# A hybrid attention layer on one core: q and k of the forgetting attention stored as two planes, high and low

## The chip, the cores and the metric

The kernel runs on one core of one Trainium2 chip. The metric is the device time of one launch in microseconds (us); smaller is better. The engines of a core that matter here are TensorE (PE; its weight loads are listed apart as PEld), VectorE (DVE), ScalarE (ACT), GpSimd (POOL) and SyncE (SP). A transfer between device memory and the core's SBUF is issued by one of the engines: `nc.sync` by SP, `nc.scalar` by ACT, `nc.gpsimd` by POOL. Matrix products accumulate in PSUM tiles of 128x512.

## The reference

One layer of a decoder with sequence length and width 1024 and float32 throughout. The cut below keeps what is computed:

```python
h = rms_norm(x, g);  proj = h @ w_in
o_a = softmax-merge over 3 groups of dilated_window_attention(...)  # 12 heads, width 64
logits = (q @ k.T) * 64**-0.5 + (c[t] - c[s]); mask s <= t           # 8 forgetting heads
o_b = softmax(logits) @ v                   # c = cumulative sum of log_sigmoid(f)
x = x + (sigmoid(gate_a) * (o_a @ w_dil_out) + sigmoid(gate_b) * (o_b @ w_fox_out)) @ w_out
x = x + (silu(h2 @ w_up1) * (h2 @ w_up2)) @ w_down                   # h2 = rms_norm(x), 2816 wide
out = rms_norm(x, g_final)
```

## The kernel before, in words

**Every product is three.** A float32 operand is held as a pair of fp32r tiles: a high part, which ScalarE makes by a copy, and a low part, which VectorE makes as the source less the high part (`split`, lines 94 to 96). A product of pairs is high times high, high times low and low times high (`mm3`, lines 98 to 101, and `prod`, line 272, whose matmul is line 276).

**Stages**, with their place in the profile. Norm, values and combinations of the normalized input's quadrants (`T1` to `T4`): up to some 137 us. **Block products**, to some 264 us: six calls of `projections` (line 279), four for q and k of the forgetting heads (a pair of heads is a block of 128 columns, and a call makes two blocks) and two for dilated heads. A call multiplies two column blocks of weights by the input with seven block products of 12 matmuls instead of eight, by the scheme of Strassen and Winograd: `left_side` (line 252) takes two raw weight tiles, `rg` and `ru` (tag `wr`, 2 buffers, loaded on SP at line 243), and makes the pairs A1 (of `rg`), S12 and S34 (from sums formed on GpSimd in tiles `s`) and A22, the second half of `ru` (tag `a22`). The products' sums are joined into two tiles `qo` (128x1024, 3 buffers), and these are stored to device memory by GpSimd (line 314), those of the forgetting heads to `fqk_dram`. The same `left_side` serves the FFN later.

**Forgetting attention**, some 290 to 503 us, two heads at a time, each in two halves of queries. `fox_qk` (line 550) makes a pair's operands: for each head, and for q and for k, it loads the head's 64 rows from `fqk_dram` twice, into rows 0 to 63 and 64 to 127 of a tile `qraw` (2 buffers; line 558, SP); ScalarE copies it to the high part (line 559; q times the factor `SCALE`), and VectorE subtracts (lines 563 and 566). `qx` then holds the high part of q in both halves, `kx` the high part of k in one half and its low part in the other, and `ql` the low part of q in one half and zeros in the other. A score is `kx`·`qx` (high and low k by high q) plus `kx`·`ql` (line 583). `fox_scores` writes logits to `L` on ScalarE (L587), takes maxima on VectorE and one over all keys on GpSimd; `fox_exp` subtracts (VectorE) and exponentiates (ScalarE); `fox_values` multiplies with the values and, by a product with ones, makes the denominators. The scores of a unit of work are issued ahead of the values of the unit before.

**Late projections** (`ahead`, line 214): 24 calls, 8 for the remaining dilated q and k (to `dqk_dram`) and 16 for the gates (to `g_dram`). A call loads 128 weight columns and splits them (`wr`, `wh`, `wl`), makes 48 products into two PSUM tiles `pf` (lines 99 to 101, tag `f`, 2 banks), copies them on ScalarE to a tile `fst` (line 224, 2 buffers), and stores that on ScalarE's queue (line 225). The last call is held behind the last value product of the dilated attention:

```python
with tc.issue_after(last_pv[0].ins) if i == 2 * KT - 1 else ExitStack():
    ahead(fpool, GATE0 + n * P, g_dram[n])
```

**Dilated attention**, some 510 to 651 us, in the same steps; its exponentials are ScalarE L750 to L756, its value products L780 and its denominators L783. **Merge**, from some 668 us: attention outputs are loaded into tiles `land` and split into `oh` and `ol` (`load_o`, by lines 95 and 96), then come the products with `w_fox_out` and `w_dil_out` (L189 and following), `w_out`, the FFN and the last norm, to the end at 1520 us.

**What sets the order.** No order is written out by hand. The program is written as a sequence of instructions, and a scheduler simulates the engines and puts each engine's instructions into one fixed order; tags and buffer numbers of the pools say what must wait for what. Products of `ahead` stand between attention steps wherever that simulation put them.

Of the kernel before, what the change touches and what calls it, by code (L numbers as in the profile page):

```python
# [8 lines left out]
F32 = mybir.dt.float32  # L9
# [6 lines left out]
P = 128  # L16
# [31 lines left out]
def layer_kernel(  # L48
# [152 lines left out]

    g_dram = dpool.tile([2 * KT, P, S], F32, name="g_dram")

    fqk_dram = dpool.tile([2, 4, P, S], F32, name="fqk_dram")
    vf_dram = dpool.tile([NT, P, FOX_W], F32, name="vf_dram")
    dqk_dram = dpool.tile([2, 3, 2, P, S], F32, name="dqk_dram")
    vd_dram = dpool.tile([3, NT, P, 256], F32, name="vd_dram")
# [38 lines left out]
    def pair_of(raw):  # L246

        w = Pair(*[wpool.tile([P, KT, P], F32R, tag="w" + n, name=nm("w" + n), bufs=2) for n in "hl"])
        split(w.hi[:], w.lo[:], raw)
        return w  # L250

    def left_side(pool, rg, ru, bufs):

        def pair(k, tag, bufs):
            return Pair(*[pool.tile([P, k, P], F32R, tag=tag + n, name=nm("w" + n), bufs=bufs) for n in "hl"])

        def fill(w, raw):
            split(w.hi[:], w.lo[:], raw)
            return w

        g1, g2, u1, u2 = rg[:, :4], rg[:, 4:], ru[:, :4], ru[:, 4:]
        S34, A22, A1 = pair(KT, "s34", 1), pair(4, "a22", 2), pair_of(rg[:])
        s12 = pool.tile([P, KT, P], F32, tag="s", name=nm("s12"), bufs=2)
        nc.gpsimd.tensor_tensor(out=s12[:, :4], in0=u1, in1=u2, op=ALU.add)  # L264
        nc.gpsimd.tensor_tensor(out=s12[:, 4:], in0=s12[:, :4], in1=g1, op=ALU.subtract)  # L265
        S12 = fill(pair(KT, "s12", bufs), s12[:])
        s34 = pool.tile([P, KT, P], F32, tag="s", name=nm("s34"), bufs=2)
        nc.gpsimd.tensor_tensor(out=s34[:, :4], in0=g1, in1=u1, op=ALU.subtract)
        nc.gpsimd.tensor_tensor(out=s34[:, 4:], in0=g2, in1=s12[:, 4:], op=ALU.subtract)
        return A1, S12, fill(S34, s34[:]), fill(A22, u2)  # L270
# [5 lines left out]
                last_mm[0] = nc.tensor.matmul(bank[:], p, q, start=first and k == 0 and n == 0,  # L276
                                              stop=k == 3 and n == 2, skip_group_check=True)

    def projections(pool, T, c, dst, dls, sc):

        T1, T2, T3, T4 = T
        o1, o2 = [pool.tile([P, dl, S // dl], F32, tag="qo", name=nm("qo"), bufs=3) for dl in dls]
# [28 lines left out]
        prod(b3, S34[:, 4:], B22)  # L311
        join(o1[:, :, n1:], b3, v2, dls[0])
        for o, d in zip((o2, o1), dst[::-1]):
            nc.gpsimd.dma_start(out=d, in_=o[:].rearrange("p r i -> p (r i)"))

    LAG = 3
    merge_order = []
# [90 lines left out]
    with pool_of("comb1", 1) as tpool:  # L408
# [90 lines left out]
        with pool_of("proj", 1) as upool:  # L499
            cums = [upool.tile([P] + d, F32, name=n, bufs=1) for n, d in (  # L500
                ("sums", [2, P]), ("az", [NT * 8]), ("u", [NT * 8]), ("t1", [NT * 8]), ("tot", [NT, 8]))]
            for pr in range(0, 4, 2):
                for a in range(2):
                    c0 = FOX0 + a * FOX_W + pr * P
                    projections(upool, T, (c0, c0 + P), [fqk_dram[a, pr + i] for i in range(2)], (1, 1), 1.0)
                if pr == 0:
                    decay(*cums)
            for two in TWOS:
                projections(upool, T, [dil_cols(*t) for t in two], [dqk_dram[t] for t in two],
                            [STR[a][g] for u, g, a in two], (SCALE, 1.0)[two[0][2]])  # L510
# [35 lines left out]
    with pool_of("fox", 1) as spool:  # L546
# [3 lines left out]
        def fox_qk(pool, ql, pr):  # L550

            qx = [pool.tile([P, S], F32R, tag=f"qx{e}", name=nm("qx"), bufs=1) for e in range(2)]
            kx = [pool.tile([P, S], F32R, tag=f"kx{e}", name=nm("kx"), bufs=1) for e in range(2)]
            for a, xs, sc in ((0, qx, SCALE), (1, kx, 1.0)):
                for e in range(2):
                    raw = pool.tile([P, S], F32, tag="qraw", name=nm("qraw"), bufs=2)
                    for at in half:
                        nc.sync.dma_start(out=raw[at, :], in_=fqk_dram[a, pr, half[e], :])
                    nc.scalar.activation(out=xs[e][:], in_=raw[:], func=AF.Copy, scale=sc)
                    rows = half[e] if a == 0 else half[1 - e]  # L560
                    hi = xs[e][rows, :].bitcast(F32)
                    if a == 0:
                        nc.vector.scalar_tensor_tensor(out=ql[e][rows, :], in0=raw[rows, :], scalar=sc, in1=hi,
                                                       op0=ALU.mult, op1=ALU.subtract)
                    else:
                        nc.vector.tensor_tensor(out=xs[e][rows, :], in0=raw[rows, :], in1=hi, op=ALU.subtract)
            return qx, ql, kx

        def fox_scores(pool, qk, h, b):
# [72 lines left out]
        with pool_of("foxa", 2) as apool:  # L642
            pend = None
            ql = [apool.tile([P, S], F32R, name=f"ql{e}", bufs=1) for e in range(2)]
            for e in range(2):
                nc.gpsimd.memset(ql[e][half[1 - e], :].bitcast(F32), 0.0)
            for pr in range(4):
                qk = fox_qk(apool, ql, pr)
                for b in range(2):
                    unit = [fox_scores(apool, qk, 2 * pr + e, b) for e in range(2)], pr, b  # L650
                    if pend:
                        fox_values(apool, *pend)
                    pend = unit
            fox_values(apool, *pend)
# [431 lines left out]
```

## Time and profile before

| | us |
|---|---|
| median of 3 runs | 1523.96 (1522.74 to 1524.77) |
| the profiled execution | 1522.51 |
| its span in the profile | 1520.2 |
| TensorE busy | 1472.8, 97% of the span |
| VectorE busy | 894.1, 59% |
| ScalarE busy | 536.8, 35% |

The profiled execution's time is 2.3 us more than its span, which is taken from the first to the last recorded instruction. The mean granted clock of TensorE is 0.992 of full speed. In the slices of 38 us below (each digit tenths of a slice; PEclk the granted clock), TensorE is full nearly throughout. The slices under 9 are the first, two that hold the end of the dilated attention and the start of the merge (608 to 684 us), and the last:

```profile
## 2 busy tenths in 40 slices
PE   7999999999999999789999999999999999999997
PEld 6899888867777777568888788888888877888886
DVE  6482433398898399936628854444444445856546
ACT  5232221476566132335315432222222225312113
POOL 1012321273353011100000155555555553140000
PEclk9999999999999999989999999999999999999999
```

### The profile page before, as it was taken

How to read it: one execution, taken by the hardware profiler on the slowest of the kernel's cores; microseconds unless marked ns; L12 is line 12 of the kernel's file. 1: busy time of each engine (PE TensorE's matmuls, PEld its weight loads, DVE VectorE, ACT ScalarE, POOL GpSimd, SP SyncE). 2: the span in 40 equal slices, each digit the busy share in tenths (PEclk: the TensorE clock that was granted, in tenths of full speed). 3: DMA queues.
4: the chain of work that ended last, by engine and by line, in shares of the span. 5: the costliest groups of instructions: out<-in, count | busy, mean ns of one | idle time of the engine just before them, and what ended most of it. 6: DMA issues, size and time to landing. Idle time of an engine off the chain costs nothing.

```text
span 1520.2 us, 18124 instructions
## 1 busy us (share of the span) xinstructions
PE 1472.8 (97%) x6956; PEld 1192.0 (78%) x6956; DVE 894.1 (59%) x1321; ACT 536.8 (35%) x808; POOL 418.4 (28%) x351
## 2 busy tenths in 40 slices
PE   7999999999999999789999999999999999999997
PEld 6899888867777777568888788888888877888886
DVE  6482433398898399936628854444444445856546
ACT  5232221476566132335315432222222225312113
POOL 1012321273353011100000155555555553140000
PEclk9999999999999999989999999999999999999999
DMA  8132334733332732155613122222222225642202
GB/s 257 42 98 63 111 97 121 226 113 102 110 99 69 257 122 66 56 181 180 242 56 139 42 69 84 83 83 83 84 83 83 84 97 197 204 139 84 96 15 97
DMA packets 139045, 171.60 MB, mean 113 GB/s; under 512 B 6992, under 2 KB 108368, under 8 KB 138960
## 3 DMA queue, kind: packets, MB, share of 16 engines
q1 hardware_dynamic: 118096, 105.95, 23.5%
q0 software_dynamic: 9616, 34.62, 6.1%
q10 hardware_dynamic: 11248, 29.89, 5.3%
q8 instruction: 54, 0.88, 0.2%
q14 instruction: 31, 0.25, 0.1%
HBM read 123.25 MB, written 47.19 MB: 112 GB/s over the span
## 4 chain that ended last, share of the span: by engine, by line
PE 85%; DMA 4%; DVE 3%; ACT 3%; POOL 3%; issue 2%; SPq 0%; ACTq 0%; POOLq 0%; DVEq 0%
PE pd L276 26%; PE pd L99 10%; PE pd L100 10%; PE pd L101 10%; PE pf L100 5%; PE pf L101 5%; PE pf L99 5%; DMA wr<-in_w_ffn_in_dram 2%; PE pd L189 2%; PE pd L634 2%; PE pd L190 2%; PE pd L193 2%; ACT wh L95 2%; POOL sg L994 1%; PE pd L780 1%
## 5 line engine op out<-in xcount | busy, mean ns | idle before, releaser
L96 DVE TENSOR_TENSOR wl<-wr,wh 128x1024 fp32r<-128x1024 f32 (+2 forms) x152 | 165.9, 1095 | 147.3 <-ACT wh L95 146.7
L95 ACT ACTIVATE wh<-wr 128x1024 fp32r<-128x1024 f32 (+2 forms) x152 | 140.6, 932 | 316.2 <-PE pd L100 91.9
L276 PE MATMUL pd<-hT_t,wh 128*128 128x512 f32 x784 | 242.2, 390 | 1.4 <-ACT cc L289 0.7
L276 PE MATMUL pd<-tT,wh 128*128 128x512 f32 x672 | 206.9, 389 | 0.4 <-DVE v L909 0.4
L276 PEld LDWEIGHTS pd<-hT_t,wh 128*128 128x128 f32 x784 | 147.0, 188 | 32.4 <-ACT c L977 1.1
L276 PE MATMUL pd<-hT_t,wl 128*128 128x512 f32 x392 | 153.9, 393 | 1.7 <-DVE wl L96 1.5
L99 PE MATMUL pf<-hT_t,wh 128*128 128x512 f32 x384 | 151.0, 393 | 0.6 <-ACT fst L224 0.6
L100 PE MATMUL pf<-hT_t,wh 128*128 128x512 f32 x384 | 151.0, 393 | 0.0
L101 PE MATMUL pf<-hT_t,wl 128*128 128x512 f32 x384 | 150.9, 394 | 0.0
L276 PEld LDWEIGHTS pd<-tT,wh 128*128 128x128 f32 x672 | 126.1, 188 | 27.0 <-DVE v L909 0.8
L99 PE MATMUL pd<-wh,wh 128*128 128x512 f32 x352 | 137.6, 392 | 3.4 <-DVE acc L1037 1.9
L100 PE MATMUL pd<-wl,wh 128*128 128x512 f32 x352 | 137.1, 389 | 0.0
L101 PE MATMUL pd<-wh,wl 128*128 128x512 f32 x352 | 137.0, 389 | 0.0
L276 PE MATMUL pd<-tT,wl 128*128 128x512 f32 x336 | 130.1, 390 | 0.0
L1037 DVE TENSOR_TENSOR acc<-pd,acc 128x512 f32<-128x512 f32 x128 | 85.6, 685 | 69.2 <-PE pd L101 69.1
L264 POOL TENSOR_TENSOR s<-wr 128x512 f32<-128x512 f32 x26 | 38.9, 1496 | 312.8 <-DVE tT L96 196.0
L96 DVE TENSOR_TENSOR wl<-s,wh 128x1024 fp32r<-128x1024 f32 x52 | 64.7, 1246 | 66.6 <-ACT wh L95 63.7
L95 ACT ACTIVATE wh<-s 128x1024 fp32r<-128x1024 f32 x52 | 55.1, 1060 | 126.5 <-POOL s L265 95.1
L276 PEld LDWEIGHTS pd<-hT_t,wl 128*128 128x128 f32 x392 | 73.6, 188 | 22.2 <-DVE wl L96 7.3
L101 PEld LDWEIGHTS pf<-hT_t,wl 128*128 128x128 f32 x384 | 72.1, 188 | 19.8 <-issue 5.0
L99 PEld LDWEIGHTS pf<-hT_t,wh 128*128 128x128 f32 x384 | 72.1, 188 | 19.7 <-issue 4.6
L100 PEld LDWEIGHTS pf<-hT_t,wh 128*128 128x128 f32 x384 | 72.1, 188 | 18.5 <-issue 4.1
(228 smaller groups left out, 2776.8 us busy)
## 6 DMA issues: line engine op xcount, KB each, us to landing
wr<-in_w_in_dram SPq DMA_DIRECT2D x46, 512.0 KB, 4.3
wr<-in_w_ffn_in_dram SPq DMA_DIRECT2D x44, 512.0 KB, 4.3
wr<-a_dram SPq DMA_DIRECT2D x22, 512.0 KB, 4.3
wr<-in_w_ffn_down_dram SPq DMA_DIRECT2D x22, 512.0 KB, 3.7
a_dram<-a POOLq DMA_DIRECT2D x20, 512.0 KB, 5.0
qraw<-fqk_dram SPq DMA_DIRECT2D x32, 256.0 KB, 4.2
g_dram<-fst ACTq DMA_DIRECT2D x16, 512.0 KB, 2.9
land<-g_dram SPq DMA_DIRECT2D x16, 512.0 KB, 3.4
```

The costliest lines, as they stand in the source:

```text
L95: nc.scalar.activation(out=hi, in_=src, func=AF.Copy)
L96: return nc.vector.tensor_tensor(out=lo, in0=src, in1=hi.bitcast(F32), op=ALU.subtract)
L99: nc.tensor.matmul(psum, w.hi, m.hi, start=start, stop=False)
L100: nc.tensor.matmul(psum, w.hi, m.lo, start=False, stop=False)
L101: last_mm[0] = nc.tensor.matmul(psum, w.lo, m.hi, start=False, stop=stop)
L189: nc.tensor.matmul(pt[hh][:], w.hi[:, k], m.hi, start=(k == 0), stop=False)
L190: nc.tensor.matmul(pt[hh][:], w.hi[:, k], m.lo, start=False, stop=False)
L193: nc.tensor.matmul(pt[hh][:], w.lo[:, k], m.hi, start=False, stop=(k == kt - 1))
L264: nc.gpsimd.tensor_tensor(out=s12[:, :4], in0=u1, in1=u2, op=ALU.add)
L276: last_mm[0] = nc.tensor.matmul(bank[:], p, q, start=first and k == 0 and n == 0, stop=k == 3 and n == 2, skip_group_check=True)
L634: nc.tensor.matmul(po[half[e], HALF - width[j]:], vf[:, j, pr, e], L[:, off[j]:off[j + 1]], start=(j == nj - 1), stop=(j == 0), skip_group ...
L1037: nc.vector.tensor_tensor(out=acc[:, t, cs], in0=pt[:], in1=acc[:, t, cs], op=ALU.add)
```

## The change

`fqk_dram` gets one more axis of length two: a plane for the high part and one for the low part. `projections`, for the four calls that make the forgetting heads' q and k, splits each finished block there: ScalarE copies it to a new tile `qh` (128x1024, 1 buffer), VectorE subtracts in place, and GpSimd stores both, one plane each. q is scaled there instead of in `fox_qk`. `fox_qk` loads parts that are ready: for each head 5 loads on ScalarE's queue, high and low k into the two halves of `kx`, high q twice into `qx`, low q into rows 0 to 63 of `ql`. The pair `a22` has one buffer instead of two in `projections`.

In counts: 32 loads on SP become 40 on ScalarE's queue; 8 stores become 16; 16 ScalarE copies and 16 VectorE subtractions leave `fox_qk`, and 8 and 8 are added in `projections`. The number of matrix products is the same, 6578.

```diff
-    fqk_dram = dpool.tile([2, 4, P, S], F32, name="fqk_dram")
+    fqk_dram = dpool.tile([2, 4, 2, P, S], F32, name="fqk_dram")
@@ left_side
-        S34, A22, A1 = pair(KT, "s34", 1), pair(4, "a22", 2), pair_of(rg[:])
+        S34, A22, A1 = pair(KT, "s34", 1), pair(4, "a22", bufs), pair_of(rg[:])
@@ projections
-    def projections(pool, T, c, dst, dls, sc):
+    def projections(pool, T, c, dst, dls, sc, hl=False):
...
-            nc.gpsimd.dma_start(out=d, in_=o[:].rearrange("p r i -> p (r i)"))
+            flat = o[:].rearrange("p r i -> p (r i)")
+            if hl:
+                hi = pool.tile([P, S], F32R, tag="qh", name=nm("qh"), bufs=1)
+                split(hi[:], flat, flat)
+                nc.gpsimd.dma_start(out=d[0], in_=hi[:].bitcast(F32))
+                nc.gpsimd.dma_start(out=d[1], in_=flat)
+            else:
+                nc.gpsimd.dma_start(out=d, in_=flat)
@@ the calls for the forgetting heads
-                    projections(upool, T, (c0, c0 + P), [fqk_dram[a, pr + i] for i in range(2)], (1, 1), 1.0)
+                    projections(upool, T, (c0, c0 + P), [fqk_dram[a, pr + i] for i in range(2)], (1, 1),
+                                (SCALE, 1.0)[a], True)
@@ fox_qk
-            for a, xs, sc in ((0, qx, SCALE), (1, kx, 1.0)):
-                for e in range(2):
-                    raw = pool.tile([P, S], F32, tag="qraw", name=nm("qraw"), bufs=2)
-                    for at in half:
-                        nc.sync.dma_start(out=raw[at, :], in_=fqk_dram[a, pr, half[e], :])
-                    nc.scalar.activation(out=xs[e][:], in_=raw[:], func=AF.Copy, scale=sc)
-                    rows = half[e] if a == 0 else half[1 - e]
-                    hi = xs[e][rows, :].bitcast(F32)
-                    if a == 0:
-                        nc.vector.scalar_tensor_tensor(out=ql[e][rows, :], in0=raw[rows, :], scalar=sc, in1=hi,
-                                                       op0=ALU.mult, op1=ALU.subtract)
-                    else:
-                        nc.vector.tensor_tensor(out=xs[e][rows, :], in0=raw[rows, :], in1=hi, op=ALU.subtract)
+            for e in range(2):
+                q, k = [fqk_dram[a, pr, :, half[e], :] for a in range(2)]
+                for to, src in ((kx, k), (qx, (q[0], q[0]))):
+                    for i in range(2):
+                        nc.scalar.dma_start(out=to[e][half[i], :].bitcast(F32), in_=src[i])
+                nc.scalar.dma_start(out=ql[e][:DH, :].bitcast(F32), in_=q[1])
@@ ahead of the loop over pairs
-                nc.gpsimd.memset(ql[e][half[1 - e], :].bitcast(F32), 0.0)
+                nc.gpsimd.memset(ql[e][DH:, :].bitcast(F32), 0.0)
```

The scheduler's order changes with it. Three places, before and then after; names carry numbers that differ from build to build, and the lines after `fox_qk` are two higher in the changed kernel.

TensorE at the end of the dilated attention: the last denominators (L783, after L785), the first of the last value products (L780, after L782) and the products of `ahead` (L99 to L101). Before, the rows follow each other without a gap:

```order
L99 MATMUL pf_5225<-hT_t,wh_5226 128x512
L783 MATMUL pd_4268<-Mx_4023,ones 64x512
L783 MATMUL pd_4268<-Mx_4022,ones 64x512
L100 MATMUL pf_5225<-hT_t,wh_5226 128x512
L101 MATMUL pf_5225<-hT_t,wl_5227 128x512
L780 MATMUL pd_4338<-L_598_4172,vd_3767 64x256
```

After, behind the same denominators:

```order
L101 MATMUL pf_5097<-hT_t,wl_5099 128x512
L785 MATMUL pd_4260<-Mx_4015,ones 64x512
L785 MATMUL pd_4260<-Mx_4014,ones 64x512
L99 MATMUL pf_5097<-hT_t,wh_5098 128x512
L100 MATMUL pf_5097<-hT_t,wh_5098 128x512
L101 MATMUL pf_5097<-hT_t,wl_5099 128x512
```

and ahead of the last values:

```order
L100 MATMUL pf_5216<-hT_t,wh_5218 128x512
L101 MATMUL pf_5216<-hT_t,wl_5219 128x512
L99 MATMUL pf_5216<-hT_t,wh_5218 128x512
L100 MATMUL pf_5216<-hT_t,wh_5218 128x512
L782 MATMUL pd_4330<-L_590_4164,vd_3759 64x256
L782 MATMUL pd_4330<-L_589_4163,vd_3759 64x256
```

Between the two stand 2 products of `ahead` before and 71 after.

ScalarE in the block products, where it splits weights (`wh<-wr`, of 128x1024 for A1 and of 128x512 for A22) and sums (`wh<-s`), and copies product sums (`cc`, `qo`). Before:

```order
L95 ACTIVATE wh_1326<-wr_1318 128x1024
L95 ACTIVATE wh_1195<-s_159_1210 128x1024
L95 ACTIVATE wh_1324<-wr_1320 128x512
L95 ACTIVATE wh_1333<-s_176_1330 128x1024
L95 ACTIVATE wh_1478<-wr_1470 128x1024
L95 ACTIVATE wh_1476<-wr_1472 128x512
L289 ACTIVATE cc_1315<-pd_1344 128x512
L95 ACTIVATE wh_1322<-s_179_1337 128x1024
L95 ACTIVATE wh_1485<-s_197_1482 128x1024
L289 ACTIVATE qo_1313<-pd_1344 128x512
```

After:

```order
L95 ACTIVATE wh_1334<-wr_1326 128x1024
L95 ACTIVATE wh_1195<-s_159_1210 128x1024
L95 ACTIVATE wh_1341<-s_178_1338 128x1024
L95 ACTIVATE wh_1494<-wr_1486 128x1024
L95 ACTIVATE wh_1332<-wr_1328 128x512
L95 ACTIVATE qh_1311<-qo_1187 128x1024
L290 ACTIVATE cc_1323<-pd_1352 128x512
L95 ACTIVATE wh_1330<-s_181_1345 128x1024
L95 ACTIVATE qh_1316<-qo_1186 128x1024
L95 ACTIVATE wh_1501<-s_201_1498 128x1024
L290 ACTIVATE qo_1321<-pd_1352 128x512
```

Before, both the second block's A22 (`wh_1324`) and the third's (`wh_1476`) are split ahead of the second block's first copy (`cc`); after, only the second's (`wh_1332`), and two splits of finished blocks (`qh`) stand among the weights.

ScalarE where the second pair's operands are made, among the logits L587 (after L589) of the first pair. Before:

```order
L587 ACTIVATE L_2118<-pd_2155,negc 128x256
L559 ACTIVATE qx_2271<-qraw_2275 128x1024
L587 ACTIVATE L_2118<-pd_2163,negc 128x128
L587 ACTIVATE L_2172<-pd_2174,negc 128x512
L95 ACTIVATE wh_3584<-wr_3586 128x1024
```

After:

```order
L589 ACTIVATE L_2140<-pd_2177,negc 128x256
L567 DMA qx_2293<-fqk_dram 64x1024
L589 ACTIVATE L_2140<-pd_2185,negc 128x128
L567 DMA kx_2295<-fqk_dram 64x1024 x2
L567 DMA qx_2293<-fqk_dram 64x1024
L589 ACTIVATE L_2194<-pd_2196,negc 128x512
L568 DMA ql_2052<-fqk_dram 64x1024
L589 ACTIVATE L_2194<-pd_2200,negc 128x512
```

The copy from `qraw` is gone; in its place ScalarE's queue issues transfers, each behind the logits that stand ahead of it.

## Rows read from the trace of the kernel before

**Rows 1.** The page: busy us (share of the span) and instructions of each engine.

```profile
PE 1472.8 (97%) x6956; PEld 1192.0 (78%) x6956; DVE 894.1 (59%) x1321; ACT 536.8 (35%) x808; POOL 418.4 (28%) x351
```

**Rows 2.** Busy time by stretch: stretch, us; busy us of PE, PEld, DVE, ACT, POOL; PEclk, DMA share, GB/s.

```profile
290.00:500.00 210.00, 206.38 (x982) 151.99 (x982) 175.68 (x302) 131.32 (x238) 91.01 (x87) 1.00 0.35 103
310.00:340.00 30.00, 26.38 (x128) 18.75 (x128) 28.38 (x44) 21.39 (x40) 20.53 (x16) 1.00 0.42 125
...
634.90:643.60 8.70, 0.00 (x0) 0.00 (x0) 8.42 (x14) 4.36 (x7) 1.78 (x1) 0.73 0.32 90
643.66:650.64 6.98, 6.98 (x64) 5.46 (x66) 2.27 (x3) 0.00 (x0) 0.00 (x0) 0.61 0.00 0
592.05:596.40 4.35, 4.35 (x65) 3.71 (x65) 4.35 (x8) 2.92 (x4) 0.00 (x0) 1.00 0.00 0
...
760.00:800.00 40.00, 40.00 (x178) 33.13 (x177) 10.63 (x13) 4.25 (x4) 0.00 (x0) 1.00 0.17 53
150.00:260.00 110.00, 110.00 (x488) 91.10 (x488) 44.10 (x58) 26.03 (x31) 30.93 (x29) 1.00 0.33 106
```

**Rows 3.** Timeline, 642 to 651 us: start, us, engine, instruction, [wait before <- releaser].

```profile
642.55 1.06 ACT L756 ACTIVATE L<-L 128x1024 f32<-128x1024 f32 x1 [0.57 <-DVE L L755]
...
643.66 7.15 PE L780 MATMUL pd<-L,vd 128*64 128x256 f32 x64 [8.78 <-ACT L L756]
```

**Rows 4.** Timeline, 662 to 669 us.

```profile
663.73 0.33 ACTq L225 DMA_DIRECT2D g_dram<-fst  x1
...
667.11 2.00 ACT L95 ACTIVATE oh<-land 128x1024 fp32r<-128x1024 f32 x2 [3.40 <-DMA g_dram<-fst]
...
668.21 1.22 PE L189 MATMUL pd<-oh,wh 128*128 128x512 f32 x2 [5.44 <-ACT oh L95]
```

**Rows 5.** Instructions on `qraw`: ns least/median/most of one, first to last start; landing times.

```profile
L559 ACT ACTIVATE qx<-qraw x8: 1047/1060/1078, 277.6 to 425.8; 128x1024 fp32r<-128x1024 f32 x8
L563 DVE SCALAR_TENSOR_TENSOR ql<-qraw,qx x8: 1208/1220/1985, 278.7 to 429.2; 64x1024 fp32r<-64x1024 f32 x8
L559 ACT ACTIVATE kx<-qraw x8: 1060/1062/1062, 284.9 to 433.6; 128x1024 fp32r<-128x1024 f32 x8
L566 DVE TENSOR_TENSOR kx<-qraw,kx x8: 1209/1220/1223, 286.0 to 434.7; 64x1024 fp32r<-64x1024 f32 x8
...
DMA to landing us min/median/max: 3.4/4.2/7.9
```

**Rows 6.** TensorE's waits, 300 to 345 us: us in total, times, longest.

```profile
PE pd L583 <- ACT L L587: 0.9, 1, 0.9
PE pd L583 <- DVE den L330: 0.8, 1, 0.8
```

**Rows 7.** Timeline, 159.5 to 171 us: the split of an A22.

```profile
162.97 0.63 ACT L95 ACTIVATE wh<-wr 128x512 fp32r<-128x512 f32 x1 [6.87 <-PE pd L276]
...
163.81 0.68 DVE L96 TENSOR_TENSOR wl<-wr,wh 128x512 fp32r<-128x512 f32 x1
```

**Rows 8.** Line L243, the raw weight loads, 137 to 262 us.

```profile
L243 SPq EVENT_SEMAPHORE  x11: 17/28/40717, 99.8 to 210.7; - x11
...
DMA to landing us min/median/max: 3.7/4.0/5.5
```

**Rows 9.** Instructions on tiles `s`, 137 to 262 us.

```profile
L95 ACT ACTIVATE wh<-s x12: 1045/1061/1063, 143.0 to 246.5; 128x1024 fp32r<-128x1024 f32 x12
L96 DVE TENSOR_TENSOR wl<-s,wh x12: 1215/1222/2317, 144.1 to 248.0; 128x1024 fp32r<-128x1024 f32 x12
...
L268 POOL TENSOR_TENSOR s<-wr,wr x5: 1288/1289/2202, 149.6 to 229.1; 128x512 f32<-128x512 f32 x5
```

**Rows 10.** Line L314, the stores of finished blocks, whole span.

```profile
L314 POOL DMA_DIRECT2D fqk_dram<-qo x8: 533/556/742, 164.2 to 227.7; - x8
...
DMA to landing us min/median/max: 2.9/3.0/8.0
```

**Rows 11.** Instructions on `dqk`, the dilated operands' loads on ScalarE's queue.

```profile
L677 ACTq DMA_DIRECT2D dqk<-dqk_dram x12: 326/442/1051, 510.9 to 551.6; - x12
```

## The prediction

> **What bounds the kernel now.** I read the page first: TensorE is busy 97% of the span [rows 1]. No number of matrix products changes here, so the edit can only give back time in which TensorE stands still or runs at its lower clock, or add such time. I therefore went to the busy time by stretch, and then to the order of time around each stretch that was not full.
>
> What a full stretch looks like: from 760 to 800 us TensorE issues 178 products of 512 columns in 40 us [rows 2], so one costs 40/178 = 0.2247 us. The gate and late dilated projections (function `ahead`, PSUM tiles `pf`) are made of just these products. Nothing in the attention waits for most of them, so the scheduler uses them as filler between attention steps: 24 calls of 48 products. I call one such product a filler.
>
> Four places matter. (1) The end of the dilated attention: from 634.9 to 643.6 us TensorE does nothing, while VectorE is busy 8.42 of 8.70 us [rows 2]. The next product, L780, comes 8.78 us late and waits for the last exponential, L756 on ScalarE [rows 3]. Its 64 records then take 6.98 us at a mean granted clock of 0.61; the same 64 one step earlier took 4.35 us at 1.00 [rows 2]. So this hole costs 8.8 + 2.6 = 11.4 us. The order of before shows why nothing fills it: 2 fillers are left between the denominators L783 and L780, and the last 48 are held until L780 has gone. (2) Right after those 48: 5.44 us of idle TensorE ahead of L189, until ScalarE splits `oh`, which itself waited for the store `g_dram<-fst` issued at 663.73 us [rows 4]. (3) The start of the forgetting attention: from 310 to 340 us TensorE is busy 26.38 of 30 us, VectorE 28.38 [rows 2]: 3.6 us lost. (4) The block products from 150 to 260 us: no loss at all, 110.00 of 110 us [rows 2].
>
> **The change part by part.** *Splits leave the attention.* 16 ScalarE copies of 1.06 us and 16 VectorE subtractions of 1.22 us go [rows 5], 17.0 and 19.5 us; 12 of the latter, 14.6 us, lie behind the first scores. TensorE gains nothing from this by itself, since it was full from filler. But from 290 to 500 us VectorE works 175.68 of 210 us [rows 2] and sets how soon the softmax steps come, so attention gets shorter and uses less filler. I counted it in the order: up to the first dilated scores 711 fillers are issued instead of 811 (26 fewer ahead of the first scores, 75 fewer up to the last denominators, one more behind them). The 100 left over, 22.5 us of work, turn up at place 1: 71 instead of 2 ahead of the last values, 79 instead of 48 behind them (69 + 31 = 100). The wait at place 1 lasts 8.78 us behind 2 fillers; 71 fillers last 16.0 us. It is covered with some 6.7 us to spare, and without the pause I expect no lower clock there: **−11.4 us**, the whole of place 1. TensorE's total work is unchanged: what it does not do early, it does there.
>
> *Place 2 stays.* More filler ahead of it does not help, since the wait hangs on the store of the last filler itself [rows 4], which still comes last: 0 us.
>
> *Place 3.* Two of its waits, 0.9 and 0.8 us, stand before the scores of the second pair (L583) [rows 6], whose tiles were still being split; the new order also puts 143 instead of 128 fillers between the first scores and the first long values. Bounds: 3.6 us back (all of it), or 4 us lost, one filler call's worth of slack being the most that a tighter order could miss. I take **−1.5 us**, near those two waits.
>
> *Splits arrive in the block products.* 8 ScalarE copies (1.06 us) and 8 VectorE subtractions over 128x1024 (some 1.23 us, by the same shape in rows 9): 8.5 and 9.8 us, where both engines have over half of 110 us free [rows 2]. 8 more GpSimd store issues of 0.556 us [rows 10], 4.4 us, where GpSimd is busy 30.93 of 110. All are off TensorE's path unless something queued behind them is late, and that is so in one case:
>
> *The `a22` buffer, 2 to 1.* To make room, the split of a block's A22 (a second half of the raw weights `ru`) must now wait until TensorE has used the A22 of the block before; so the `ru` buffer comes free one block later, and the next block's `ru` is loaded later. The chain from the end of that product: ScalarE split and VectorE remainder end 1.5 us on [rows 7]; load 4.0 us, 3.7 to 5.5 [rows 8]; three GpSimd additions, 1.29 each [rows 9]; ScalarE 1.06 and VectorE 1.22 for the sum S12 [rows 9]: 1.5 + 4.0 + 3.9 + 1.1 = 10.5 us to S12's high part, 11.7 to the low one. The new order leaves 49 products between A22 and the next S12 (53 the first time) before the high part is due, 11.0 us, and 4 more, 11.9 us, before the low one. So this chain, which had blocks to spare, now just fits. It comes 4 times. Bounds: 0 at the median landing; at 5.5 us some 1.3 us each, 5.2 us. The two stores of the block, 512 KB each, now run beside the load, so I take a landing near 5 us: some 0.75 us each, **+3.0 us**.
>
> *Loads.* 32 issues on SP become 40 on ScalarE's queue. The dilated operand loads from the same queue take 0.326 to 1.051 us, median 0.442 [rows 11]: 40 x 0.442 = 17.7 us in place of the 17.0 us of copies; 13 to 42 at the ends. ScalarE is busy 131.32 of 210 us from 290 to 500 [rows 2], so either end fits: 0 us. A pair's loads are queued behind the last scores of a head, and some 12 us of other products stand before they are needed, against a landing of 4.2 us, 7.9 at worst [rows 5]: 0 us. SP loses 32 issues that stood between the filler's weights: 0 us.
>
> **Sum:** −11.4 − 1.5 + 3.0 = −9.9 us. The profiled execution took 1522.51 us (span 1520.2 and 2.3 around it), so 1512.6; the median, 1523.96, lies 1.45 above it: **1514.0 us**. With the ends of the two unknown terms, −15.0 to −2.2 us: 1509.0 to 1521.8, most of it below 1519.
>
> **Rivals.** *A, place 2 goes as well.* For it: attention is over earlier relative to the filler. Against: the store that is waited for is the last filler's own [rows 4]. It would give back 5.4 us: 1508.6. Chance 0.10.
>
> *B, the block products become bound by the weight load.* For it: the chain above has under 0.5 us to spare. Against: it needs more than the worst landing of those weights. Place: the S12 products of the third to sixth block. With the worst landing of any store of that line, 8.0 us [rows 10], and one addition at 2.2 us [rows 9], S12's low part comes at 16.6 instead of 11.9 us: 4.7 x 4 = 18.8 us, −11.4 − 1.5 + 18.8 = +5.9: 1529.9. It turns the sign from (11.4 + 1.5)/4 = 3.2 us a block, a landing of about 7.4 us. Chance 0.05.
>
> *C, ScalarE is held by the loads.* The loads wait in ScalarE's own queue, ahead of evictions: SP's queue shows a single wait of 40.7 us before a load [rows 8], harmless there. Here TensorE runs out of `pf` banks 24 fillers, 5.4 us, after an eviction stops. A hold of 7.9 us [rows 5] loses 2.5 us; at 8 groups of loads 20 us: 1534.0. The Trainium skill, DMA: Bandwidth & Descriptors, section Anatomy of one DMA — SWDGE (gpsimd) path, has it as a rule that any semaphore wait of a transfer happens on the issuing sequencer before dispatch; by that rule each late load stops ScalarE, and the 40.7 us wait agrees. Against it: the loads' conditions are the same products that the next eviction waits for. Chance 0.04.
>
> *D, the attention can't be pressed that much.* The order takes 16.9 us (75 fillers) out of the stretch from the first scores to the last denominators; VectorE loses 14.6 us, so its share of the stretch stays at 161/193 = 83%, as 176/210 is now. If half of the 16.9 comes back as TensorE waiting for exponentials, −9.9 + 8.5: 1522.6, no difference. Chance 0.08.
>
> **How the numbers follow.** 0.2% of this time is 3 us, about what a measurement of this kernel can tell from no change. The forecast has 0.73 and A 0.10, both faster by more; D, 0.08, is no change; B and C, 0.09, are slower. Faster 0.83, same 0.08, slower 0.09. The range runs from A's 1508.6 less the 2.1 us by which place 3 may give more, 1506.5, to the upper end of the forecast at 1521.8; D, B and C lie outside, 0.17.
>
> **What would show it.** In the profile after: no wait of L782 (L780 before) for the last exponential over 1 us, its 64 records in about 4.4 us at clock 1.00, with filler ahead; still 5.4 us before L189; TensorE in the block products short by 1 to 5 us, waiting for `wh` or `wl` of S12; the stretch from 290 us to the last denominators some 17 us shorter with at most 4 us idle. Wrong if the idle time at L782 is still there, if the waits at S12 exceed 3 us each, or if `pf` products wait for `fst` evictions that stand behind a load.

## The result and the profile after

The changed kernel takes 1528.7 us, median of 5 runs (1526.24 to 1532.95), against 1523.69 us (1522.74 to 1524.77) before: a ratio of 1.0036, 95% interval 1.0018 to 1.0053. It is slower by 5 us where 1514.0 was forecast. The profiled execution took 1528.70 us, its span is 1527.0 us, 6.8 us more than before.

The page of the changed kernel, to be held against the slices shown ahead:

```profile
PE   7999999699999999989999999999999999999997
...
PEclk9999999799999999999999999999999999999999
```

TensorE's work is the same, 1473.1 us busy for 1472.8. The 17th digit, with the end of the dilated attention, was 7 and is now 9: the hole that the forecast rests on is gone. The 18th stays 8; it holds the wait at the start of the merge. But the eighth digit, 267 to 305 us, has fallen from 9 to 6, its clock to 0.7. The readings need the stretches in numbers; columns as in [rows 2]:

```profile
150.00:260.00 110.00, 107.25 (x472) 87.54 (x471) 58.01 (x67) 33.59 (x39) 36.65 (x37) 1.00 0.43 144
280.00:306.00 26.00, 12.26 (x43) 9.61 (x42) 1.23 (x1) 2.63 (x4) 0.00 (x0) 0.67 0.72 181
...
638.00:647.70 9.70, 9.70 (x46) 7.75 (x44) 7.16 (x10) 4.72 (x7) 0.00 (x0) 1.00 0.17 56
647.74:652.00 4.26, 4.26 (x67) 3.68 (x68) 0.00 (x0) 0.00 (x0) 0.00 (x0) 1.00 0.20 60
```

The block products now lose 2.75 of 110 us; the last exponentials of the dilated attention are covered by fillers; the last 64 values run at clock 1.00. And from 280 to 306 us TensorE stands still for more than half the time, and ScalarE is busy 2.63 of 26 us. TensorE's waits there, 262 to 312 us (us in total, times, longest):

```profile
PE pf L99 <- ACT fst L225: 13.7, 1, 13.7
```

A filler's first product waits for a PSUM bank that ScalarE has to copy out (`fst`, L225). What ScalarE does is in its timeline (ACT is the engine, ACTq its queue of transfers):

```profile
271.17 0.58 ACT L225 ACTIVATE fst<-pf 128x512 f32<-128x512 f32 x1
271.78 0.34 ACTq L226 DMA_DIRECT2D dqk_dram<-fst  x1
272.15 1.17 ACTq L567 DMA_DIRECT2D kx<-fqk_dram  x2
273.35 1.77 ACTq L567 DMA_DIRECT2D qx<-fqk_dram  x2
275.15 0.62 ACTq L568 DMA_DIRECT2D ql<-fqk_dram  x1
275.80 5.00 ACTq L567 DMA_DIRECT2D kx<-fqk_dram  x2
292.51 1.10 ACTq L567 DMA_DIRECT2D qx<-fqk_dram  x2
...
294.31 0.60 ACT L225 ACTIVATE fst<-pf 128x512 f32<-128x512 f32 x1 [22.56 <-issue]
```

These are nine of the ten operand loads of the first pair, one behind the other; the last, `ql`, follows at 293.66 us. The eighth, high q of the second head, is issued only at 292.51 us, and the eviction of `pf` stands behind it. The releaser that the profile names, "issue", means that no compute instruction explains the wait. The transfers issued from 268 to 284 us explain it (transfer, queue, count, KB, median us to landing):

```profile
vf<-vf_dram POOLq DMA_DIRECT2D x1, 2048.0 KB, 18.4
...
dqk_dram<-fst ACTq DMA_DIRECT2D x1, 512.0 KB, 8.5
wr<-in_w_in_dram SPq DMA_DIRECT2D x1, 512.0 KB, 19.5
```

The weight load `wr`, issued by SP at 273.02 us, lands 19.5 us later, at 292.49; the load that ScalarE held was issued at 292.51. A semaphore is a counter that tells when a transfer has landed. In the trace the transfers of SP and ScalarE carry eight semaphore numbers in turn; these two carry the same one, 113, and the later one waits on it before it is issued. Likewise the load issued at 280.35 us carries 112, the number of the `fst` store which landed at 280.33. So ScalarE waited for a transfer that has nothing to do with attention, because of a number that the two share. After the wait 38 products take 11.40 us, at a mean clock of 0.75, where 8.5 are due.

### The profile page after: what moved, and what is told of

It reads as the page before. It is cut to its first block, busy times and chain, and to the rows that moved or that the text cites. A ratio compares the mean times of both kernels' runs of the same rounds, so it can differ in the third digit from the quotient of the medians.

```text
span 1527.0 us, 18126 instructions
## 1 busy us (share of the span) xinstructions
PE 1473.1 (96%) x6956; PEld 1192.3 (78%) x6956; DVE 890.4 (58%) x1313; ACT 528.2 (35%) x800; POOL 406.0 (27%) x359
## 4 chain that ended last, share of the span: by engine, by line
PE 82%; DMA 5%; DVE 4%; ACT 4%; POOL 3%; issue 1%; ACTq 0%; SPq 0%; POOLq 0%; DVEq 0%
PE pd L277 24%; PE pd L99 10%; PE pd L100 10%; PE pd L101 10%; PE pf L99 5%; PE pf L100 5%; PE pf L101 5%; DMA wr<-in_w_ffn_in_dram 2%; ACT wh L95 2%; DMA wr<-in_w_in_dram 2%; PE pd L189 2%; PE pd L193 2%; PE pd L636 2%; PE pd L190 2%; DVE wl L96 2%; POOL sg L996 1%
## 5 line engine op out<-in xcount | busy, mean ns | idle before, releaser
L99 PE MATMUL pf<-hT_t,wh 128*128 128x512 f32 x384 | 153.4, 400 | 14.3 <-ACT fst L225 14.3
L100 PE MATMUL pf<-hT_t,wh 128*128 128x512 f32 x384 | 152.4, 397 | 0.0
L101 PE MATMUL pf<-hT_t,wl 128*128 128x512 f32 x384 | 152.0, 396 | 0.0
L99 PE MATMUL pd<-wh,wh 128*128 128x512 f32 x352 | 137.3, 391 | 3.1 <-DVE acc L1039 1.7
L101 PE MATMUL pd<-wh,wl 128*128 128x512 f32 x352 | 136.9, 389 | 0.0
L99 PEld LDWEIGHTS pf<-hT_t,wh 128*128 128x128 f32 x384 | 73.1, 190 | 35.4 <-ACT fst L225 15.1
L101 PEld LDWEIGHTS pf<-hT_t,wl 128*128 128x128 f32 x384 | 73.0, 190 | 17.1 <-issue 2.1
```

Source lines behind the costliest of these rows:

```text
L99: nc.tensor.matmul(psum, w.hi, m.hi, start=start, stop=False)
L100: nc.tensor.matmul(psum, w.hi, m.lo, start=False, stop=False)
L101: last_mm[0] = nc.tensor.matmul(psum, w.lo, m.hi, start=False, stop=stop)
```

## The experiments

Theory Q: the loss sits in ScalarE's queue, held by a semaphore shared with a late transfer. Theory T: it is traffic, and TensorE would wait whatever queue issues the loads. Ratios are to the kernel before as it ran beside each experiment on the same chip, 1521 to 1522 us.

**The loads on SP** (`sp_loads`):

```diff
-                        nc.scalar.dma_start(out=to[e][half[i], :].bitcast(F32), in_=src[i])
-                nc.scalar.dma_start(out=ql[e][:DH, :].bitcast(F32), in_=q[1])
+                        nc.sync.dma_start(out=to[e][half[i], :].bitcast(F32), in_=src[i])
+                nc.sync.dma_start(out=ql[e][:DH, :].bitcast(F32), in_=q[1])
```

> The changed kernel with the ten operand loads of each pair issued by SP (as before the change) instead of ScalarE; the scheduler's order stays the same up to the first scores (134 filler products ahead of them). Theory Q (the loss sits in ScalarE's queue: a load of the second head waits there for a late transfer, and the eviction of pf behind it stops TensorE): the 13.7 us wait of TensorE for fst at 281 us and the 2.8 us at a lower clock behind it go, 1528.7 - 16.5 = about 1512. Theory T (the loss is the traffic: too much is under way at 268 to 292 us, and whatever queue issues the loads, TensorE must wait for operands or for the filler's weights): at least 8 of the 16.5 us stay, as waits of the first scores or of a filler's first product, 1520 or more.

Measured: 1512.19 us, ratio 0.9937 (0.9922 to 0.9952). SP meets the same kind of hold and ScalarE none; first SP's queue, then ScalarE's:

```profile
278.77 1.32 SPq L567 DMA_DIRECT2D kx<-fqk_dram  x2
284.41 1.32 SPq L567 DMA_DIRECT2D qx<-fqk_dram  x2
```

```profile
275.59 0.60 ACT L225 ACTIVATE fst<-pf 128x512 f32<-128x512 f32 x1 [4.07 <-PE pf L101]
```

SP waits 4.3 us for the weight load (landing 11.6 us here), and nothing that TensorE needs soon stands behind it. TensorE's waits from 262 to 312 us are 1.3 us for `qx` and 0.3 for `ql`. The share of busy transfer engines from 268 to 292 us is 0.95 here and 0.92 in the changed kernel. Q holds so far, though the weight load landed sooner here than in the changed kernel, so the traffic was not quite the same. By the sum the rest of the change is worth what was forecast, 0.9937 of 1523.69 is 1514.1; its terms are not: counted from mark to mark as in the part on the prediction, the block products cost 5.1 us here and the forgetting attention gives back 2.9. The scheduler's order behind the first scores differs a little as well.

**vf later** (`vf_late`): the changed kernel, loads on ScalarE; `first_s` holds the first `affine_select` of `fox_scores`.

```diff
-        nc.gpsimd.dma_start(out=vf[:].rearrange("p t a b d -> p t (a b d)"), in_=vf_dram.rearrange("t p c -> p t c"))
...
+                    if not pend:
+                        with tc.issue_after(first_s[0].ins):
+                            nc.gpsimd.dma_start(out=vf[:].rearrange("p t a b d -> p t (a b d)"),
+                                                in_=vf_dram.rearrange("t p c -> p t c"))
```

> The changed kernel with the 2 MB load of the values, vf, issued behind the first causal mask of the forgetting attention instead of at 270 us; the operand loads stay on ScalarE's queue. Theory Q with the late transfer as its cause: the weight load that took 19.5 us lands within some 10, the hold on ScalarE is at most 9 us less the 5.4 us that the pf banks cover, so 0 to 4 us of the 16.5 stay: 1512 to 1516. Theory T says the same here: traffic is gone. If ScalarE is held whatever the traffic (the loads' own buffers come free late), the wait for fst stays over 10 us: 1525 or more. The order has 96 instead of 134 filler products ahead of the first scores, so a wait of 1 to 3 us of the first score for its operands may show.

Measured: 1508.54 us, 0.9919 (0.9902 to 0.9935). ScalarE's queue in that run:

```profile
275.05 1.25 ACTq L568 DMA_DIRECT2D kx<-fqk_dram  x2
278.03 1.10 ACTq L568 DMA_DIRECT2D qx<-fqk_dram  x2
...
279.82 0.60 ACT L225 ACTIVATE fst<-pf 128x512 f32<-128x512 f32 x1 [8.52 <-DMA kx<-fqk_dram]
```

The weight load now lands 5.9 us after its issue, at 278.01; the same load of `qx` leaves at 278.03. The hold is 1.7 us and from 262 to 312 us TensorE waits for nothing longer than 0.5 us. With `vf_late_oh` below this is the fastest median measured, and it beats both kernels. It lies 3.5 us under the 1512 to 1516 that were expected. In the traces 3.0 us of what it gains beyond the hold are in the dilated attention, where the changed kernel has 3.4 us at a granted clock of 0.50 (from 536.1 us) and this one none.

**Three loads on GpSimd** (`three_on_pool`): same bytes, same shapes, `vf` early; three loads go to another queue, and so the semaphores that the transfers carry change.

```diff
+                dma = nc.gpsimd if pr == 0 and e == 1 else nc.scalar
...
-                        nc.scalar.dma_start(out=to[e][half[i], :].bitcast(F32), in_=src[i])
-                nc.scalar.dma_start(out=ql[e][:DH, :].bitcast(F32), in_=q[1])
+                        (nc.scalar if to is kx else dma).dma_start(out=to[e][half[i], :].bitcast(F32), in_=src[i])
+                dma.dma_start(out=ql[e][:DH, :].bitcast(F32), in_=q[1])
```

> The changed kernel with three of the first pair's ten loads, high and low q of the second head, issued by GpSimd, whose transfers use semaphores of their own; shapes, bytes and vf as in the change. ScalarE's queue then keeps 7 loads, the last of which waits for the store of a fst that landed at 280.3 us in the changed kernel, and none meets the semaphore of the slow weight load (292.5 us). If that shared semaphore is what held ScalarE, its next eviction runs from about 281 us, the 13.7 us wait for fst is at most 1 us, and the time is about 1512, with the weight load still late, 11 us or more. If ScalarE's queue is held by slow transfers as such, 8 us or more of the wait stay: 1520 or more.

Measured: 1515.28 us, 0.9950 (0.9934 to 0.9966). The same three views as above, transfers issued from 268 to 284 us, ScalarE, and TensorE's waits from 262 to 312 us:

```profile
wr<-in_w_in_dram SPq DMA_DIRECT2D x1, 512.0 KB, 22.8
```

```profile
277.17 5.15 ACTq L568 DMA_DIRECT2D kx<-fqk_dram  x2
282.36 0.60 ACT L225 ACTIVATE fst<-pf 128x512 f32<-128x512 f32 x1 [9.17 <-DMA dqk_dram<-fst]
...
283.80 0.59 ACT L225 ACTIVATE fst<-pf 128x512 f32<-128x512 f32 x1
297.35 0.33 ACTq L226 DMA_DIRECT2D dqk_dram<-fst  x1
```

```profile
PE pd L586 <- ACT L L590: 1.3, 1, 1.3
PE pf L99 <- ACT fst L225: 1.2, 2, 0.8
```

The weight load is even later, 22.8 us, and yet the wait for `fst` is 1.2 us instead of 13.7. Traffic alone does not stop TensorE; the shared semaphore ahead of an eviction does. The expectation was wrong in one point: number 113 held ScalarE here as well. The `fst` store issued at 297.35 us carries it, and the weight load landed at 297.27, so ScalarE did nothing for 13 us. But by then it had copied out both banks (282.36 and 283.80 us), and TensorE went on with fillers and scores. A hold costs little behind the evictions and 13.7 us ahead of one. It is not free: the first scores, made at 291.76 us, were read by ScalarE only from 298.22, a wait of 0.8 us for `fst` stands right behind the hold, and the time is 3 us above the expected 1512.

**Both** (`sp_vf_late`), the two diffs together.

> The operand loads on SP and vf behind the first mask, both at once. If the queue of the loads costs something only while the weight load is late, this equals the kernel with vf moved alone, 1508.5, within 2 us. If loads on ScalarE's queue cost something at the later pairs too, this is faster by 3 us or more.

Measured: 1512.5 us, 0.9936 (0.9919 to 0.9952), 4 us above `vf_late` in the medians, with intervals of the ratios that overlap. So no run shows that loads on ScalarE's queue cost anything at the later pairs. The 2 us of the expectation were not met; in the two traces most of the difference lies in the forgetting attention, in another order of the same work, and why that order is no faster stays open.

**One buffer for a22 alone** (`before_a22_one`): the kernel before with

```diff
-        S34, A22, A1 = pair(KT, "s34", 1), pair(4, "a22", 2), pair_of(rg[:])
+        S34, A22, A1 = pair(KT, "s34", 1), pair(4, "a22", bufs), pair_of(rg[:])
```

> The kernel before with one buffer for a22 in the block products, nothing else changed: the prediction's chain term by itself. If the chain is the cause of the waits for wh and wl of S12 at 144, 196 and 218 us in the changed kernel, they show here as well, 1 to 1.4 us each, 4 to 5 us in all; the rival, that the splits and stores added to the block products delay S12 on ScalarE, VectorE and GpSimd, expects none here. The order now has 14 instead of 2 filler products ahead of the last values, which should shorten the 8.8 us wait there by 2.7 us. Sum: 1523.7 + 4.5 - 2.7 = about 1525.5 by the chain, 1521 by the rival.

Measured: 1528.34 us, 1.0044 (1.0029 to 1.0059). TensorE's waits from 142 to 262 us, of the changed kernel first:

```profile
PE pd L277 <- DVE wl L96: 2.3, 2, 1.2
PE pd L277 <- ACT wh L95: 1.5, 2, 1.1
```

```profile
PE pd L276 <- ACT wh L95: 1.3, 2, 1.1
PE pd L276 <- ACT cc L289: 0.7, 1, 0.7
PE pd L276 <- DVE wl L96: 0.5, 3, 0.2
```

(The 0.7 for `cc`, at 141 to 142 us, stands in all three kernels.) By these lists the buffer alone seems to cost little at the later blocks, 0.2 us at a time. But the end of a product is modelled, and a list of idle time leaves out what TensorE loses while the products behind a wait start up again. From the start of one product to the next are 0.227 us when nothing waits. Counted so, the breaks of the kernel with one buffer are 1.8 us at 145 us and 0.4, 0.8, 0.9 and 0.9 us at 178, 196, 217 and 237 us; the kernel before has 0.3 us, at 145. The later four are the chain of the prediction, about 0.75 us each. GpSimd waits for the raw weights, whose load was issued at 186.92 us, behind the split of the block's A22 at 185.37:

```profile
191.87 1.28 POOL L264 TENSOR_TENSOR s<-wr 128x512 f32<-128x512 f32 x1 [1.79 <-DMA wr<-in_w_in_dram]
```

The break at 145 us comes with the one buffer too, though not by the chain, since no block stands ahead of it: the split of S12 stands on ScalarE behind an activation of the forget gates' decay, which now waits 2.8 us for VectorE instead of 1.3. The changed kernel has the break at 145 us, none at 178 and 237, and 2.1 and 1.7 us at 196 and 217. Its timeline shows what was added, GpSimd's additions and then VectorE:

```profile
190.12 1.29 POOL L265 TENSOR_TENSOR s<-wr 128x512 f32<-128x512 f32 x1 [1.59 <-DMA wr<-in_w_in_dram]
191.38 1.28 POOL L269 TENSOR_TENSOR s<-wr,wr 128x512 f32<-128x512 f32 x1
192.63 2.27 POOL L266 TENSOR_TENSOR s<-s,wr 128x512 f32<-128x512 f32 x1
```

```profile
192.09 1.66 DVE L96 TENSOR_TENSOR qo<-qo,qh 128x1024 f32<-128x1024 f32 x1 [2.02 <-ACT qh L95]
196.03 2.34 DVE L96 TENSOR_TENSOR wl<-s,wh 128x1024 fp32r<-128x1024 f32 x1 [2.27 <-ACT wh L95]
```

The subtraction that the change brought and GpSimd's addition run at the same time, and both are slow: 2.27 us for 1.29, 1.66 for 1.23. The addition ahead of the break at 217 us takes 2.27 us too; at the two blocks without a break it takes 1.29 and 1.28. So both guesses hold in part: the one buffer makes the chain tight, and the added work makes it late. The rest of the loss of the kernel with one buffer lies elsewhere: it has waits of 1.0 to 1.5 us for `fst` and for operands in the forgetting attention, and still 6.9 us at the last values; 12 more fillers there, 2.7 us of work, took only 1.9 us off the wait.

**vf later in the kernel before** (`before_vf_late`), the same edit as in `vf_late`.

> The kernel before with the load of vf issued behind the first causal mask. Its order differs from before in this: 137 instead of 160 filler products ahead of the first scores, and 49 instead of 2 ahead of the last values. If what the wait at the last values needs is filler ahead of it and nothing else, 49 products (11.0 us) cover the 8.8 us wait and the clock does not fall behind it, so 11.4 us go without any split leaving the attention: about 1512. If the wait there is bound by VectorE's work of the attention as a whole, 5 us or more of it stay: 1517 or more.

Measured: 1516.85 us, 0.9976 (0.9966 to 0.9986). The wait at the last values is 1.9 us, and their 64 records take 4.24 us from first to last start, as in the changed kernel, against 6.92 before. So filler ahead of the last values is what counts, with or without splits in the attention. It is worth 9.5 us there; two new waits ahead of scores, 4.0 us in all, take back part of it. Over the kernels, wait and filler ahead: 8.8 us behind 2, 6.9 behind 14, 1.9 behind 49, none behind 71. The 1.9 us are not for want of filler, though. VectorE was done for the last exponential (L762) at 638.1 us, but on ScalarE a filler's weight split stood ahead of it, and that had to wait for the fillers on TensorE:

```profile
639.36 0.63 ACT L95 ACTIVATE wh<-wr 128x512 fp32r<-128x512 f32 x1 [1.81 <-PE pf L100]
...
640.37 1.05 ACT L762 ACTIVATE L<-L 128x1024 f32<-128x1024 f32 x1
```

**oh not over fst** (`sp_oh_moved`; `vf_late_oh` is the same edit with `vf_late`):

```diff
-            if br == 1:
+            if br == 1 and dt > 2:
                 ms[dt] = mpool.tile([P, S], F32, tag="m", name=nm("m"), bufs=LAG + 2)
...
+        ms = {dt: mpool.tile([P, S], F32, tag="m", name=nm("m"), bufs=LAG + 2) for dt in range(3)}
         load_o(1, 2, 4)
-        ms = {}
```

> The kernel with the operand loads on SP, and with three tiles m of the merge allocated ahead of oh, so that oh no longer lies where fst lay. If the 5.4 us wait ahead of L189 is oh waiting for the store of the last fst, some 3 us of it go (the copy of the last fst, 0.6 us, and the split of oh, 1.06, still stand ahead of L189 on ScalarE): 1512.2 - 3 = about 1509. If the wait is for the attention output's own loads, nothing changes.

> Both moves on the changed kernel, vf loaded behind the first mask and oh not over fst, with the operand loads on ScalarE as in the change: 1508.5 - 3 = about 1505.5 if the two are independent; 1508.5 if the wait ahead of L189 is for something else than the store.

Measured: 1510.05 us, 0.9921 (0.9906 to 0.9936), and 1508.76 us, 0.9917 (0.9899 to 0.9934). The first products of L189 wait 2.5 instead of 5.4 us in both, so the wait was for memory where `fst` lay, as the forecast said. In the times this can't be told from nothing: in both profiled executions the part behind L189 is 3.8 to 3.9 us longer than without the edit. In both the clock falls to half twice behind L189, at the same two places, and in the profiles of the two kernels without the edit it does not. Of the first kernel, columns as in [rows 2]:

```profile
831.40:834.80 3.40, 3.40 (x11) 2.72 (x11) 3.37 (x4) 0.60 (x1) 0.00 (x0) 0.50 0.00 0
1282.00:1285.40 3.40, 3.40 (x10) 2.62 (x9) 3.40 (x5) 1.06 (x1) 0.00 (x0) 0.51 0.48 153
```

Two times half of 3.4 us are 3.4 us, most of what is given back. Only one execution of each kernel was profiled, so whether it comes each time, and whether the edit brings it, was not settled.

**Fewer loads** (`few_loads`; `all_moved` adds the edits of `vf_late_oh`):

```diff
-                for to, src in ((kx, k), (qx, (q[0], q[0]))):
-                    for i in range(2):
-                        nc.scalar.dma_start(out=to[e][half[i], :].bitcast(F32), in_=src[i])
+                nc.scalar.dma_start(out=kx[e][:].bitcast(F32), in_=k)
+                nc.scalar.dma_start(out=qx[e][:].bitcast(F32), in_=q[0].unsqueeze(0).broadcast_to([2, DH, S]))
```

> The changed kernel with 3 loads for each head instead of 5, on ScalarE's queue as in the change and with the same bytes: both planes of k in one transfer, and high q into both halves in one. All transfers of SP and ScalarE take turns on eight semaphores, and one that takes a semaphore waits for the transfer that had it eight before. With 6 loads for the first pair none of them meets the semaphore of the slow weight load. If the hold comes from that shared semaphore, the 13.7 us wait for fst goes although the traffic of 268 to 292 us is the same: about 1512, as with the loads on SP. If it comes from ScalarE's queue being full of slow transfers, 10 us or more of it stay: 1522 or more.

> Three moves on the changed kernel: 3 loads for each head instead of 5, vf behind the first mask, oh not over fst. If the hold of ScalarE by the shared semaphores still costs anything with vf moved, this is faster than the same without the fewer loads; since there the loads waited for no semaphore longer than 3 us, I expect no difference: about 1505.5.

Measured: 1634.03 us, 1.0737 (1.0721 to 1.0753), and 1642.57 us, 1.0786 (1.0768 to 1.0804). Both missed, and the runs don't test the semaphores, since the edit changed the transfers themselves. ScalarE's queue, and a stretch of 20 us:

```profile
274.58 15.72 ACTq L567 DMA_DIRECT2D ql<-fqk_dram  x1
...
291.45 10.36 ACTq L566 DMA_DIRECT2D qx<-fqk_dram  x1
301.86 10.13 ACTq L567 DMA_DIRECT2D ql<-fqk_dram  x1
```

```profile
292.00:312.00 20.00, 0.00 (x0) 0.00 (x0) 0.00 (x0) 0.00 (x0) 0.00 (x0) 0.50 0.14 53
```

With transfers written as two planes of 64 rows a share of 0.14 of the transfer engines is busy, some two of the 16, and they move 53 GB/s, by which 512 KB take 9.9 us. Three of the issuing instructions, one such load and two of `ql` behind them, last 10 to 16 us, and hold ScalarE as long. The clean test of the semaphores became `three_on_pool`.

## Why the prediction was wrong

The terms can be held against the two traces by counting from mark to mark: how much later or earlier TensorE starts the second mark after the first, less 0.2247 us for each filler that the order moved in or out between them.

| from the mark above to | before: us, fillers | after: us, fillers | net | forecast |
|---|---|---|---|---|
| last block product (from the start) | 264.5, 48 | 268.1, 40 | +5.4 | +3.0 |
| first scores | 25.6, 112 | 38.2, 94 | +16.6 | 0 |
| last denominators, forgetting attention | 212.9, 577 | 192.2, 502 | −3.9 | −1.5 |
| denominators ahead of the last values | 130.6, 365 | 132.3, 366 | +1.5 | 0 |
| denominators behind the last values | 17.0, 2 | 21.1, 71 | −11.4 | −11.4 |
| first product of L189 | 17.6, 48 | 24.6, 79 | +0.1 | 0 |
| end | 852.0, 0 | 850.4, 0 | −1.7 | 0 |

- **The end of the dilated attention, −11.4 us: right.** No wait is left ahead of L782, and 6.92 − 4.24 = 2.7 us of slow values are gone. The forgetting attention did get shorter, by 20.7 us, where the order's 75 fillers said 16.9; rival D did not come.
- **The wait ahead of L189, 0: right**, 5.44 us as in [rows 4].
- **The start of the forgetting attention, −1.5: right in sign, too small.** In its first 59 us TensorE is busy 57.67 us; the same 59 us of before had 55.38: −2.3. Over the whole forgetting attention it is −3.9.
- **The block products, +3.0: the mechanism right, the size too small.** The listed waits went from 0.7 to 4.5 us; counted from start to start the loss is 5.4 us, just over the upper bound of 5.2. The chain by itself was priced well: where the one buffer is the only change, its four breaks are 3.0 us. There the late weight tile `ru` landed in 4.8 to 5.3 us beside the block's stores, near 5 as forecast. Two things were missing: the break at 145 us, and the added subtraction, which together with GpSimd's additions ran slow. In the changed kernel, which stores in another order, `ru` landed in 3.7 us, and the slow additions, not the load, made up the delay.
- **"Loads ... 0 us": this step failed.** It bounded the issues by their own duration and the landing by 7.9 us [rows 5], and took the loads to wait only for the products that use their buffers. The eighth load waited for a weight load that took 19.5 us, and the eviction waited with it: 13.7 us, and 11.4 − 8.5 = 2.9 at the lower clock, 16.6 us. Two things stood in the trace of before: SP's queue there waited up to 40.7 us before a load [rows 8], and the 7.9 us, against a median of 4.2, was a sign of traffic at just that time. Moving the loads to an engine that evicts made such a wait count. The prediction's own last sign of being wrong, `pf` products that wait for evictions behind a load, is what the trace shows.
- **Rival C named this place of waiting** but priced a hold at 7.9 us and 2.5 us of loss, and got 0.04, since "the loads' conditions are the same products that the next eviction waits for". One hold of 11.7 us on top of 4.0 did it, not eight. The rule of the Trainium skill that stood there (DMA: Bandwidth & Descriptors, Anatomy of one DMA — SWDGE (gpsimd) path: waits happen on the issuing sequencer before dispatch) is what this run shows, on ScalarE's queue.

The +1.5 and −1.7 that no term had foreseen are mostly the clock: the changed kernel has 3.4 us at 0.50 from 536.1 us, the kernel before 3.4 us at 0.50 from 843.7, each in one profiled execution. They nearly cancel. Unrounded the column is +6.8 us, as the spans say; the medians say 5.0. Without the failed step it is −9.9, the forecast's sum to the tenth, and the loads on SP measured 0.9937, −9.6 us. That agreement is partly luck: the block products cost 2.4 us more than forecast, and the forgetting attention gave 2.4 us more.

## What to carry to other kernels

Before moving transfers to the queue of an engine that also evicts PSUM, ask what each of them may have to wait for before it is issued, including transfers of other queues that share its semaphore, and how long the evictor can be held until TensorE runs out of banks. Where many loads start together, look at what else is in flight just then: moving one 2 MB load out of that moment was worth at least as much as choosing the queue (0.9919 and 0.9937, with intervals that overlap), and both together were worth no more. Filler ahead of a known late wait shortens it by somewhat less than its own length, however it gets there, as long as its own splits and copies do not stand ahead of the late work on another engine. And what a wait costs is read from the starts of the products around it, not from the list of waits alone: 5.4 us in the block products where the lists said 4.5.

## What the runs showed of the hardware

- A transfer that carried the semaphore number of an earlier one was issued only when that one had landed, also from another queue: 292.51 us behind a landing at 292.49, 297.35 behind 297.27, 278.03 behind 278.01.
- A weight load took 19.5 and 22.8 us when operand loads went out on another queue beside it, and 11.6 us when the same loads stood behind it on its own queue, with a share of 0.88 to 0.95 of the transfer engines busy from 268 to 292 us in all three. With `vf` moved away it took 5.9 us.
- With transfers shaped as two planes of 64 rows the rate was 53 GB/s, and the issues of one such load and of two behind such loads held ScalarE for 10.1 to 15.7 us.
- Subtractions on VectorE and additions on GpSimd that overlapped took 1.66 to 2.34 and 2.27 us in place of 1.23 and 1.29.
